# Starting the first products on the unnormed x, three-pass low-rank products, shorter token mixes and interleaved first FFN pairs in a one-layer hybrid encoder

## Chip, cores and metric

One core of a Trainium2 chip (trn2). The metric is the device time of one execution in microseconds (us). Three runs of the kernel before the change took 849.54 us in the median (849.13 to 849.97). A difference of under 0.2% (1.7 us) can't be told from no change here.

## The reference

One layer on x of 512 positions by 1024 channels, in float32: a norm, one input projection whose columns feed four mixers and their gates, an output projection, and a feed-forward network (FFN) with a width-3 convolution. Cut to what the change touches:

```python
def rms_norm(x, g):
    return x * rsqrt(mean(x * x, axis=-1) + 1e-6) * g

def rwkv7_mixer(z, mu, w0, w2, a0, a2, g2, ...):
    z = z + (token_shift(z) - z) * mu          # token_shift: the row of the position before
    r, k, v, xw, xa, xg = split(z)             # 256, 256, 256, 64, 64, 128 columns
    decay = exp(-c * sigmoid(w0 + tanh(xw) @ w2))
    a = sigmoid(a0 + xa @ a2)
    g = sigmoid(xg) @ g2
    ...
def layer(x):
    h = rms_norm(x, mix_norm_g)
    proj = h @ w_in                            # 1024 x 7424
    x = x + mixers_and_gates(proj) @ w_o
    h2 = rms_norm(x, ffn_norm_g)
    up = causal_dwconv(h2 @ w_up, conv_w)      # three taps over positions
    gate, val = split(up)
    return x + (silu(gate) * val) @ w_down
```

## The kernel before

Activations stand in SBUF transposed, channels on the partitions and the 512 positions on the free axis, in tiles of 128 positions. Every large product is float32 by three passes of fp32r: each operand is split into a rounded part and its rest (`split`: ScalarE casts the first, VectorE subtracts for the second), and `mm3` issues hi by hi, hi by rest, rest by hi into one PSUM bank. Weights come in pieces of 128 x 512 (raw, then `whi` and `wlo`) on SyncE's DMA queue, in rings of a few buffers. A unit is 1024 rows by 256 weight columns: four pieces, two banks, 48 products of 512 columns. TensorE's order is written by hand. Side work (norms, the RWKV part, attention) runs as generators that `tick()` advances, one step per some number of `mm3` calls; the constants YA, YN, Y0, WN, WO are these numbers.

The start: `load_x` brings x in tiles x0 to x3 of 128 positions. Twelve warm-up products (L232) run on TensorE. ScalarE sums the squares of a tile (L239), VectorE makes 1/rms and a diagonal matrix of it, and TensorE multiplies x by the diagonal (L300), which turns and norms at once; VectorE multiplies by the norm's gain (L248, `hf`), `split` makes hH and hL. Only then do the products of the first units begin, on positions 0 to 255 (256 columns): the unit of the low-rank inputs, that of k and r, that of v. Tiles 2 and 3 are normed on ScalarE, turned (L348) and split in between, and the units' products on positions 256 to 511 follow into the other half of the same banks (`first_units`). L366 and L367 turn the small vectors, L368 copies them out of PSUM.

The token mix (`mixed`) copies a bank out by ScalarE, and VectorE takes the difference of neighbouring positions and adds mu times it. The low-rank products (L464, L466, L468 in `rwkv_half`) are plain float32: two of 64 rows and one of 128, for each of two halves of the RWKV channels.

The FFN: of the four tiles normed by `norm_to_h`, the last goes through a diagonal product (L219) and the others through transposes (L221). `up_pair` computes a gate and a value column block, the first pair on positions 0 to 255 and then 256 to 511, the others at 512 columns. `conv` reads each bank three times: ScalarE (L1097), then VectorE (L1098 and L1099). Four banks of the kind `mm` serve these products in turn, so that pair n+2 needs the banks of pair n.

Of the kernel before, what the change touches and what calls it, by code (L numbers as in the profile page):

```python
# [9 lines left out]
F32 = mybir.dt.float32  # L10
# [5 lines left out]
P = 128  # L16
# [35 lines left out]
def hybrid_encoder_layer(  # L52
# [150 lines left out]
    def norm_to_h(np_, xs, gb, st, tt, early, wait=1, tag="mm"):  # L203

        ss, sq, xn = st
        rs = norm_factor(ss)
        if early:
            dg = np_.tile([P, P], F32, tag="diag", name="diag", bufs=2)
            vec.tensor_scalar(out=dg, in0=ident, scalar1=rs, scalar2=None, op0=ALU.mult)
        else:  # L210
            for hf in range(2):
                vec.scalar_tensor_tensor(out=xn[:, half_of(hf)], in0=xs[:, half_of(hf)], scalar=rs, in1=gb[hf], op0=ALU.mult, op1=ALU.mult)
        yield wait
        for half in range(2):
# [10 lines left out]
    def gain(xn, xs, gb, hf):  # L225
        vec.tensor_tensor(out=xn[:, half_of(hf)], in0=xs[:, half_of(hf)], in1=gb[hf], op=ALU.mult)
# [8 lines left out]
    mix_rs, mix_pt = {}, {}  # L235

    def mix_sums(tt):
        ss, sq, _ = norm_start(npool)
        act.activation(out=sq, in_=x0[tt], func=AF.Square, accum_out=ss[:, 0:1])  # L239
        return ss  # L240

    def mix_factor(tt, ss):
        mix_rs[tt] = norm_factor(ss, 1)

    def mix_gain(tt, half):

# [43 lines left out]
    sp.dma_start(out=stackB, in_=fcw[0:P])  # L290
    with tc.manual_schedule(engines={mybir.EngineType.PE, mybir.EngineType.Activation, mybir.EngineType.DVE}):
        for tt in range(2):
            mix_factor(tt, mix_sums(tt))
            dg = npool.tile([P, P], F32, tag="diag", name="diag", bufs=2)
            vec.tensor_scalar(out=dg, in0=ident, scalar1=mix_rs[tt], scalar2=None, op0=ALU.mult)
            for half in range(2):
                mix_pt[tt, half] = pt = bank()
# [893 lines left out]
```

## Time and profile before

| | before |
|---|---|
| median of 3 runs | 849.54 us |
| the profiled execution | 849.13 us |
| its span on the chip | 847.4 us |
| TensorE busy | 838.4 us, 99% of the span |
| VectorE busy | 516.4 us, 61% |
| ScalarE busy | 378.3 us, 45% |
| DMA | 82.19 MB, 97 GB/s |

The span leaves 1.73 us of the execution around it. Busy shares are averages over the whole span; the engine whose share is near 100% sets the time, and only the stretches in which it waits, and its own work, can change it.

### The profile page before, as it was taken

The page shows a single profiled execution, that of the slowest core. Times are in us where ns is not written, and L with a number is a line of the kernel's source. Part 1 is how long each engine was busy: PE and PEld are TensorE (multiplying, and loading weights), DVE is VectorE, ACT ScalarE, POOL GpSimd, SP SyncE. Part 2 cuts the span into 40 slices and gives each one's busy share as a digit, 9 for nine tenths or more (in the row PEclk, how much of TensorE's full clock was granted, in tenths as well). Part 3 has the DMA queues.
Part 4 walks back from the last instruction along what each step waited for, and adds up shares of the span by engine and source line. Part 5 has one row for each costly group of instructions (what it writes and reads, how often), then busy time and mean ns, then how long its engine had stood idle before and what let it go on. Part 6 is the DMA issues. An engine that isn't in the chain of part 4 may idle for free.

```text
span 847.4 us, 12633 instructions
## 1 busy us (share of the span) xinstructions
PE 838.4 (99%) x4759; PEld 697.2 (82%) x4759; DVE 516.4 (61%) x890; ACT 378.3 (45%) x646; POOL 11.7 (1%) x53
## 2 busy tenths in 40 slices
PE   8999999999999999999999999999999999999997
PEld 8988888788878888888888888888888888888886
DVE  5577974796466577754565866626665366634645
ACT  6474444752326554534344554405442244413434
POOL 2000100000000000000000000000000000000000
PEclk9999999999999999999999999999999999999999
DMA  8323331224213322263355333305332153302102
GB/s 252 114 63 100 106 101 51 63 79 114 65 54 98 100 62 75 87 211 100 97 169 182 113 112 99 100 1 187 99 100 63 61 165 99 100 26 66 46 1 99
DMA packets 102772, 82.19 MB, mean 97 GB/s; under 512 B 12716, under 2 KB 91640, under 8 KB 102712
## 3 DMA queue, kind: packets, MB, share of 16 engines
q1 hardware_dynamic: 101880, 79.56, 31.5%
q10 hardware_dynamic: 752, 1.58, 0.6%
q8 instruction: 37, 0.61, 0.3%
q0 software_dynamic: 80, 0.26, 0.1%
q14 instruction: 23, 0.19, 0.1%
HBM read 78.88 MB, written 2.49 MB: 96 GB/s over the span
## 4 chain that ended last, share of the span: by engine, by line
PE 95%; DVE 2%; ACT 1%; DMA 1%; issue 1%; ACTq 0%; DVEq 0%
PE mm L178 26%; PE mm L179 26%; PE mm L180 25%; PE wk L179 3%; PE wk L180 3%; PE wk L178 3%; PE wk L596 1%; PE wk L968 1%; PE wk L1000 1%; PE wk L990 1%; DMA x<-in_x_dram 0%; PE wk L540 0%; DMA raw<-in_w_down_dram 0%; PE wk L566 0%; PE wk L683 0%
## 5 line engine op out<-in xcount | busy, mean ns | idle before, releaser
L109 ACT CAST whi<-raw 128x512 fp32r<-128x512 f32 x272 | 166.7, 622 | 306.4 <-PE mm L179 178.8
L106 DVE TENSOR_TENSOR wlo<-raw,whi 128x512 fp32r<-128x512 f32 x276 | 187.1, 687 | 156.9 <-ACT whi L109 155.0
L178 PE MATMUL mm<-hH,whi 128*128 128x512 f32 (+1 forms) x432 | 166.4, 385 | 0.5 <-ACT hH L318 0.5
L179 PE MATMUL mm<-hL,whi 128*128 128x512 f32 (+1 forms) x432 | 161.6, 374 | 0.3 <-DVE hL L106 0.3
L180 PE MATMUL mm<-hH,wlo 128*128 128x512 f32 (+1 forms) x432 | 161.8, 374 | 0.0
L179 PE MATMUL mm<-h2L,whi 128*128 128x512 f32 (+1 forms) x368 | 139.9, 380 | 0.5 <-DVE h2L L106 0.5
L178 PE MATMUL mm<-h2H,whi 128*128 128x512 f32 (+1 forms) x368 | 140.0, 380 | 0.0
L180 PE MATMUL mm<-h2H,wlo 128*128 128x512 f32 (+1 forms) x368 | 139.8, 380 | 0.0
L178 PEld LDWEIGHTS mm<-hH,whi 128*128 128x128 f32 x432 | 81.3, 188 | 15.8 <-ACT hH L318 0.7
L180 PEld LDWEIGHTS mm<-hH,wlo 128*128 128x128 f32 x432 | 81.3, 188 | 14.9
L179 PEld LDWEIGHTS mm<-hL,whi 128*128 128x128 f32 x432 | 81.4, 188 | 14.3 <-DVE hL L106 0.5
L179 PEld LDWEIGHTS mm<-h2L,whi 128*128 128x128 f32 x368 | 69.2, 188 | 13.7 <-DVE h2L L106 0.7
L178 PEld LDWEIGHTS mm<-h2H,whi 128*128 128x128 f32 x368 | 69.2, 188 | 13.1
L180 PEld LDWEIGHTS mm<-h2H,wlo 128*128 128x128 f32 x368 | 69.2, 188 | 13.1
L180 PE MATMUL mm<-whi,aL 128*128 128x512 f32 (+1 forms) x92 | 35.5, 386 | 0.0
L178 PE MATMUL mm<-whi,aH 128*128 128x512 f32 (+1 forms) x92 | 35.5, 385 | 0.0
L179 PE MATMUL mm<-wlo,aH 128*128 128x512 f32 (+1 forms) x92 | 35.4, 385 | 0.0
L1098 DVE SCALAR_TENSOR_TENSOR ga<-mm,vecs,ga 128x511 f32<-128x511 f32 x22 | 16.5, 750 | 29.3 <-ACT ga L1097 29.3
L180 PE MATMUL wk<-whi,aL 128*128 128x512 f32 (+1 forms) x88 | 33.8, 385 | 0.0
L179 PE MATMUL wk<-wlo,aH 128*128 128x512 f32 (+1 forms) x88 | 33.8, 384 | 0.0
L178 PE MATMUL wk<-whi,aH 128*128 128x512 f32 (+1 forms) x88 | 33.8, 384 | 0.0
L1066 DVE TENSOR_TENSOR xt<-xt,mm 128x512 f32<-128x512 f32 x16 | 11.0, 688 | 31.9 <-PE mm L180 31.9
(336 smaller groups left out, 1169.3 us busy)
## 6 DMA issues: line engine op xcount, KB each, us to landing
raw<-in_w_in_dram SPq DMA_DIRECT2D x104, 256.0 KB
raw<-in_w_up_dram SPq DMA_DIRECT2D x176, 128.0 KB
raw<-in_w_down_dram SPq DMA_DIRECT2D x44, 256.0 KB
raw<-in_w_o_dram SPq DMA_DIRECT2D x16, 256.0 KB
x<-in_x_dram SPq DMA_DIRECT2D x4, 512.0 KB
raw<-in_w_in_dram SPq DMA_DIRECT2D x16, 128.0 KB
xt<-in_x_dram SPq DMA_DIRECT2D x4, 512.0 KB
out_dram<-xn SPq DMA_DIRECT2D x7, 256.0 KB
```

The costliest lines, as they stand in the source:

```text
L106: vec.tensor_tensor(out=lo, in0=src, in1=hi.bitcast(F32), op=ALU.subtract)
L109: act.copy(hi, src)
L178: pe.matmul(ps, lhsT=sh, rhs=mh, start=first, stop=False)
L179: pe.matmul(ps, lhsT=sh, rhs=ml, start=False, stop=False)
L180: pe.matmul(ps, lhsT=sl, rhs=mh, start=False, stop=last)
L596: pe.matmul(ps[us, i * 64:i * 64 + 64], lhsT=lt, rhs=rh, start=True, stop=True)
L968: pe.matmul(zb[b][:, o:o + QW[ti]], lhsT=qS[j][:, hp, ti * P:(ti + 1) * P], rhs=k_[j][:, hp, 0:QW[ti]], start=n == 0 and ti != 0, stop=n = ...
L990: pe.transpose(out=ab[b][:, o:o + P], in_=az[:, QOF[ti] + si * P:QOF[ti] + (si + 1) * P], identity=ident)
L1000: pe.matmul(po[:, si * P:T], lhsT=vS[j][:, hp, si, :], rhs=a_[:, cols], start=(si == 0 and n == 0), stop=(si == 3 and n == 1))
L1066: vec.tensor_tensor(out=xt[:, tt, half_of(hf)], in0=xt[:, tt, half_of(hf)], in1=bk, op=ALU.add)
L1098: vec.scalar_tensor_tensor(out=t0[:, 1:T], in0=ps[:, 0:T - 1], scalar=ffc(1, i), in1=t0[:, 1:T], op0=ALU.mult, op1=ALU.add)
```

## The change

- x comes in halves of 512 channels, the first weight pieces between them. TensorE turns the tiles x0 and x1 as they come (L254); ScalarE multiplies by the gain while it casts (`first_hi`), VectorE makes the rest (`first_lo`): fH and fL, without the norm. The first three units' products on positions 0 to 255 use these. The first two units go pass by pass (`one_pass`), the order of the units is low-rank, v, then k and r.
- The factors 1/rms of x0 and x1 come later: two products of ones by the diagonals (L406) lay them out as a row over 256 positions, L407 copies the row, and six VectorE multiplications (L410) scale the left halves of the six banks in place. x0 to x3 are normed in place, turned (L395) and split for all later units. There are seven warm-up products instead of twelve.
- The mix is one ScalarE instruction (scale 1 - mu, from PSUM) and one VectorE instruction (mu times the neighbour, from PSUM).
- The low-rank products become three passes of fp32r with split operands (L507, L509); those of the second half move into the first half's step that waits YA. Their weights are loaded by SyncE with the small vectors.
- The FFN's last tile is turned by transposes like the others, with a wait of its own (WO2), and the first two pairs run interleaved at 256 columns on all four banks (`first_pairs`).

```diff
-YN = 5
+YN = 7
 YV = 4
-Y0 = 8
-WN = 20
-WN2 = 10
+Y0 = 10
+WN = 17
+WN2 = 4
+WN3 = 12
+WN4 = 8
+WN5 = 4
 ND = 3
 FN = 4
-NWARM = 12
+NWARM = 7
 WO = 10
+WO2 = 20
...
+    for tt in range(2):
+        load_x(tt, half_of(0))
...
+    fH = npool.tile([P, KT, 256], F32R, name="fH")
+    fL = npool.tile([P, KT, 256], F32R, name="fL")
...
+    def mix_norm(tt):
+        ss = small.tile([P, 4], F32, tag="ss", name="ss")
+        sq = npool.tile([P, D], F32, tag="sq", name="sq", bufs=1)
         act.activation(out=sq, in_=x0[tt], func=AF.Square, accum_out=ss[:, 0:1])
-        return ss
-
-    def mix_factor(tt, ss):
-        mix_rs[tt] = norm_factor(ss, 1)
-
-    def mix_gain(tt, half):
-
-        hf_ = npool.tile([P, 4, P], F32, tag="hf", name="hf", bufs=4)
-        vec.tensor_tensor(out=hf_, in0=mix_pt[tt, half].rearrange("p (k t) -> p k t", k=4),
-                          in1=gT_mix[:, half * 4:half * 4 + 4, :].broadcast_to([P, 4, P]), op=ALU.mult)
...
+    def first_turn(q):
+        pt = bank("wk")
+        for k in range(2):
+            for tt in range(2):
+                kt = 2 * q + k
+                pe.transpose(out=pt[:, (2 * k + tt) * P:(2 * k + tt + 1) * P], in_=x0[tt][:, kt * P:(kt + 1) * P], identity=ident)
+        return pt
+
+    def first_hi(pt, q, k):
+        kt = 2 * q + k
+        act.activation(out=fH[:, kt, :], in_=pt[:, 256 * k:256 * k + 256], func=AF.Copy, scale=gT_mix[:, kt, :])
+
+    def first_lo(pt, q, k):
+        kt = 2 * q + k
+        vec.scalar_tensor_tensor(out=fL[:, kt, :], in0=pt[:, 256 * k:256 * k + 256], scalar=gT_mix[:, kt, :], in1=fH[:, kt, :].bitcast(F32), op0=ALU.mult, op1=ALU.subtract)
...
-    first = col_unit(w_in_v, RW0 + 768, get=load_piece)
+    first = col_unit(w_in_v[:, 0:KT // 2], RW0 + 768, get=load_piece)
+    for tt in range(2):
+        load_x(tt, half_of(1))
+    first += col_unit(w_in_v[:, KT // 2:KT], RW0 + 768, get=load_piece)
     wslots[:] = [(wA, NRA, NWA)]
-    second = col_unit(w_in_v[:, 0:KT // 2], RW0 + 256, RW0, get=load_piece)
+    second = col_unit(w_in_v, RW0 + 512, get=load_piece)
+    wslots[:] = [(npool, 8, 8)]
+    third = col_unit(w_in_v[:, 0:KT // 2], RW0 + 256, RW0, get=load_piece)
     load_x(2)
-    second += col_unit(w_in_v[:, KT // 2:KT], RW0 + 256, RW0, get=load_piece)
     load_x(3)
-    wslots[:] = [(npool, 8, 8)]
-    third = col_unit(w_in_v, RW0 + 512, get=load_piece)
+    third += col_unit(w_in_v[:, KT // 2:KT], RW0 + 256, RW0, get=load_piece)
...
+    def one_pass(n, u, ps, h):
+
+        wn, m = ((0, fH), (0, fL), (1, fH))[n]
+        for kt in range(2 * h, 2 * h + 2):
+            for ci in range(2):
+                pe.matmul(ps[ci][:, 0:256], lhsT=u[h][wn][:, kt % 2, ci * P:(ci + 1) * P], rhs=m[:, kt, :], start=n == 0 and kt == 0, stop=n == 2 and kt == KT - 1)
+                if n == 2:
+                    tick()
...
+        u, ps = unit_w[0], unit_ps[0]
+        pt = [first_turn(0), first_turn(1)]
+        first_hi(pt[0], 0, 0)
+        act.copy(w[0][1], w[0][0])
+        first_hi(pt[0], 0, 1)
+        vec.tensor_copy(w[1][1], w[1][0])
+        for k in range(2):
+            first_hi(pt[1], 1, k)
+        for h in range(2):
+            one_pass(0, u, ps, h)
+        for q in range(2):
+            for k in range(2):
+                first_lo(pt[q], q, k)
+        pt += [first_turn(2), first_turn(3)]
+        for h in range(2):
+            one_pass(1, u, ps, h)
+        for h in range(2):
+            lo_of(*w[h])
+        for h in range(2):
+            one_pass(2, u, ps, h)
...
+    def mix_rest():
+        for tt, wait in ((2, WN), (3, WN2), (0, WN3), (1, WN4)):
+            yield wait
...
+            turned.append(tt)
+            if tt == 3:
+                mix_norm(0)
+                mix_norm(1)
+        yield WN5
+        pr = bank("wk")
+        for tt in range(2):
+            pe.matmul(pr[:, tt * P:(tt + 1) * P], lhsT=ones_f, rhs=mix_dg[tt], start=True, stop=True)
+        vec.tensor_copy(rs_row, pr[:, 0:256])
+        for ps in unit_ps:
+            for bk in ps:
+                vec.tensor_tensor(out=bk[:, 0:256], in0=bk[:, 0:256], in1=rs_row, op=ALU.mult)
...
+        u, ps = unit_w, unit_ps
+        for h in range(0, 4, 2):
+            for n in range(3):
+                for i in range(2):
+                    one_pass(n, u[1], ps[1], h + i)
         ps.append([bank("wk"), bank("wk")])
-        gemm2_part(u[2], ps[2], 0)
+        gemm2_part(u[2], ps[2], 0, h=(fH, fL))
+        while len(turned) < 2:
+            finish("norm", 1)
...
-        zs = rp.tile([P, T + 1], F32, tag="zs", name="zs", bufs=2)
-        pool.memset(zs[:, 0:1], 0.0)
-        act.copy(zs[:, 1:T + 1], ps)
-        d = rp.tile([P, T], F32, tag="zd", name="zd")
-        vec.tensor_tensor(out=d, in0=zs[:, 0:T], in1=zs[:, 1:T + 1], op=ALU.subtract)
+
         zm = rp.tile([P, T], F32, tag=nm, name=nm, bufs=bufs)
-        vec.scalar_tensor_tensor(out=zm, in0=d, scalar=col("mu", mi), in1=zs[:, 1:T + 1], op0=ALU.mult, op1=ALU.add)
+        act.activation(out=zm, in_=ps, func=AF.Copy, scale=keep_mu[:, mi:mi + 1])
+        vec.scalar_tensor_tensor(out=zm[:, 1:T], in0=ps[:, 0:T - 1], scalar=col("mu", mi), in1=zm[:, 1:T], op0=ALU.mult, op1=ALU.add)
...
-        pw = bank("wk")
-        pe.matmul(pw, lhsT=w2a2[0:64, cj], rhs=lora[0:64, :], start=True, stop=True)
-        pa = bank("wk")
-        pe.matmul(pa, lhsT=w2a2[64:P, cj], rhs=lora[64:P, :], start=True, stop=True)
-        pg = bank("wk")
-        pe.matmul(pg, lhsT=g2[:, cj], rhs=xg, start=True, stop=True)
...
+            pw, pa, pg = bank("wk"), bank("wk"), bank("wk")
+            for n, (a, b) in enumerate(((0, 0), (0, 1), (1, 0))):
+                for ps, rows_ in ((pw, slice(0, 64)), (pa, slice(64, P))):
+                    pe.matmul(ps, lhsT=lw[rows_, a, cj], rhs=lx[rows_, b, :], start=n == 0, stop=n == 2)
+            for n, (a, b) in enumerate(((0, 0), (0, 1), (1, 0))):
+                pe.matmul(pg, lhsT=lw[:, 2 + a, cj], rhs=lx[:, 2 + b, :], start=n == 0, stop=n == 2)
...
+        if j == 0:
+            lora_products(1)
...
-            spawn("norm", norm_to_h(fpool, xt[:, tt, :], gb, sts[tt], tt, tt == NT - 1, WO))
+            spawn("norm", norm_to_h(fpool, xt[:, tt, :], gb, sts[tt], tt, WO2 if tt == NT - 1 else WO, "mm" if tt < 2 else "wk"))
...
+    def first_pairs():
+
+        wslots[:] = [inA] * 7 + [inB]
+        n_piece[0] = 0
+        u = [up_cols(i) for i in range(2)]
+        ps = [[bank(), bank()] for _ in range(2)]
+        for n in range(2):
+            gemm2_part(u[n], ps[n], 0)
+        finish("norm")
+        for hs in ((0, 1), (2, 3)):
+            for n in range(2):
+                gemm2_part(u[n], ps[n], 1, hs)
+        return ps
...
+        begun = first_pairs() if a == 0 else []
         for i in range(n):
             wslots[:] = [inA]
-            up_pair(a + i)
+            up_pair(a + i, begun[i] if i < len(begun) else gemm2(up_cols(a + i)))
```

**VectorE at the place where the small vectors are copied out.** Names: hf is a turned tile times the gain, hL its rest, wlo the rest of a weight piece. Before:

```order
L248 TENSOR_TENSOR hf_425<-wk_420,gT_mix_111 128x512 [waits PE_49]
L106 TENSOR_TENSOR wlo_726<-raw_724,whi_725 128x512 [waits DMAHW2_49,Activation_49]
L106 TENSOR_TENSOR hL_94<-hf_416,hH_93 128x4x128 [waits Activation_49]
L106 TENSOR_TENSOR hL_94<-hf_425,hH_93 128x4x128 [waits Activation_49]
L106 TENSOR_TENSOR wlo_732<-raw_730,whi_731 128x512 [waits DMAHW3_49]
L106 TENSOR_TENSOR wlo_738<-raw_736,whi_737 128x512 [waits DMAHW4_49]
L368 COPY vecs_288<-wk_485 128x256 [waits PE_49]
```

After, the same place:

```order
L397 TENSOR_TENSOR hf_532<-wk_527,gT_mix_106 128x512 [waits PE_49]
L397 TENSOR_TENSOR hf_541<-wk_536,gT_mix_106 128x512 [waits PE_49]
L110 TENSOR_TENSOR hL_94<-hf_532,hH_93 128x4x128 [waits Activation_49]
L110 TENSOR_TENSOR wlo_773<-raw_771,whi_772 128x512 [waits DMAHW2_49,PE_49,Activation_49]
L110 TENSOR_TENSOR hL_94<-hf_541,hH_93 128x4x128 [waits Activation_49]
L407 COPY rs_row_110<-wk_557 128x256 [waits PE_49]
L428 COPY vecs_320<-wk_567 128x256 [waits PE_49]
L410 TENSOR_TENSOR mm_189<-mm_189,rs_row_110 128x256 [waits DVE_49]
L410 TENSOR_TENSOR mm_190<-mm_190,rs_row_110 128x256
L410 TENSOR_TENSOR mm_191<-mm_191,rs_row_110 128x256
L410 TENSOR_TENSOR mm_192<-mm_192,rs_row_110 128x256
```

Here the split of tile x1 (the first five rows), the copies and the multiplications of the banks stand in one queue; two more multiplications, of wk_373 and wk_374, follow.

**TensorE at the same place**, in the second halves of the first units (mm_296 and mm_297 before; mm_191 and mm_192 after are the banks of v). Before:

```order
L180 MATMUL mm_296<-hH_93,wlo_114 128x256
L367 MATMUL wk_485<-ident_88,stackB_182 128x128 [waits DMAHW1_49]
L178 MATMUL mm_296<-hH_93,whi_113 128x256
L179 MATMUL mm_296<-hL_94,whi_113 128x256
L180 MATMUL mm_296<-hH_93,wlo_114 128x256
```

After:

```order
L395 MATMUL wk_536<-ident_88,x0_86 128x128 x3
L182 MATMUL mm_192<-hH_93,whi_130 128x256
...
L182 MATMUL mm_191<-hH_93,whi_134 128x256
...
L406 MATMUL wk_557<-diag_436,ones_f_77 128x128 [waits DVE_49]
L406 MATMUL wk_557<-diag_446,ones_f_77 128x128
...
L427 MATMUL wk_567<-ident_88,stackB_183 128x128 [waits DMAHW3_49]
L182 MATMUL mm_192<-hH_93,whi_134 128x256 [waits DVE_49]
```

Between the last transpose of tile x1 and the row that waits for VectorE stand 12 products of 256 columns (6 into mm_192, 6 into mm_191), the two factor products and the two vector transposes. What that last row waits for is the multiplication of mm_192.

**VectorE and TensorE at the first FFN pairs** (mm_4895, mm_4896 are pair 0's banks; mm_4897, mm_4898 pair 1's; mm_5207, mm_5208 pair 2's, the same memory as pair 0's; wlo_5285, 5292, 5299 belong to pair 3; before, mm_4836 and mm_4837 are pair 0's banks). VectorE before:

```order
L106 TENSOR_TENSOR wlo_5109<-raw_5107,whi_5108 128x512 [waits PE_49,Activation_49]
L1098 SCALAR_TENSOR_TENSOR ga_4970<-mm_4836,vecs_288,ga_4970 128x511 [waits Activation_49]
L106 TENSOR_TENSOR wlo_5116<-raw_5114,whi_5115 128x512 [waits DMAHW1_49,DMAHW2_49,PE_49,Activation_49]
L1099 SCALAR_TENSOR_TENSOR ga_4970<-mm_4836,vecs_288,ga_4970 128x510 [waits DVE_49]
L1098 SCALAR_TENSOR_TENSOR va_4975<-mm_4837,vecs_288,va_4975 128x511 [waits Activation_49]
L1099 SCALAR_TENSOR_TENSOR va_4975<-mm_4837,vecs_288,va_4975 128x510 [waits DVE_49]
```

VectorE after:

```order
L110 TENSOR_TENSOR wlo_5285<-raw_5283,whi_5284 128x512 [waits DMAHW0_49,DMAHW1_49,PE_49,Activation_49]
L1148 SCALAR_TENSOR_TENSOR ga_5127<-mm_4895,vecs_320,ga_5127 128x511 [waits Activation_49]
L110 TENSOR_TENSOR wlo_5292<-raw_5290,whi_5291 128x512 [waits DMAHW2_49,DMAHW3_49,PE_49,Activation_49]
L1149 SCALAR_TENSOR_TENSOR ga_5127<-mm_4895,vecs_320,ga_5127 128x510 [waits DVE_49]
L1148 SCALAR_TENSOR_TENSOR va_5132<-mm_4896,vecs_320,va_5132 128x511 [waits Activation_49]
L110 TENSOR_TENSOR wlo_5299<-raw_5297,whi_5298 128x512 [waits DMAHW4_49,DMAHW5_49,PE_49,Activation_49]
L1149 SCALAR_TENSOR_TENSOR va_5132<-mm_4896,vecs_320,va_5132 128x510 [waits DVE_49]
```

TensorE after:

```order
L184 MATMUL mm_4896<-h2H_4551,wlo_4862 128x256
L182 MATMUL mm_4897<-h2H_4551,whi_4882 128x256
...
L184 MATMUL mm_4898<-h2H_4551,wlo_4890 128x256
L182 MATMUL mm_5207<-h2H_4551,whi_5180 128x512 [waits DVE_49,Activation_49]
...
L182 MATMUL mm_5208<-h2H_4551,whi_5180 128x512 [waits DVE_49,Activation_49]
```

VectorE has one more split between pair 0's two last reads; between pair 0's last product and pair 2's first one TensorE has 24 products of 256 columns, where pair 1's whole unit (48 products of 512 columns) stood before between pair 0's and pair 2's.

## Rows read from the trace of the kernel before

**Rows 1.** The page: busy time of each engine, and TensorE's granted clock in 40 slices.

```profile
PE 838.4 (99%) x4759; PEld 697.2 (82%) x4759; DVE 516.4 (61%) x890; ACT 378.3 (45%) x646; POOL 11.7 (1%) x53
PEclk9999999999999999999999999999999999999999
```

**Rows 2.** TensorE's waits: line waited for, us in total, times, longest.

```profile
PE wk L232 <- DVE ones_f L86: 1.3, 1, 1.3
PE mm L178 <- ACT hH L318: 0.5, 1, 0.5
PE mm L179 <- DVE h2L L106: 0.5, 1, 0.5
PE mm L179 <- DVE hL L106: 0.3, 1, 0.3
```

**Rows 3.** Timeline of the start: start us, us, engine, line, out<-in, count, idle before.

```profile
1.25 5.44 PE L232 MATMUL wk<-ones_f 128*128 128x128 f32 x24 [1.25 <-DVE ones_f L86]
4.88 1.06 ACT L239 ACTIVATE sq<-x 128x1024 f32<-128x1024 f32 x1 [1.95 <-DMA x<-in_x_dram]
7.17 3.84 PE L300 MATMUL mm<-diag,x 128*128 128x128 f32 x32 [0.32 <-DVE diag L295]
11.54 0.38 PE L178 MATMUL mm<-hH,whi 128*128 128x256 f32 x1 [0.54 <-ACT hH L318]
12.27 0.39 PE L179 MATMUL mm<-hL,whi 128*128 128x256 f32 x1 [0.34 <-DVE hL L106]
```

**Rows 4.** Windows: stretch, us, busy of PE, PEld, DVE, ACT, POOL, granted clock.

```profile
12.27:48.37 36.10, 36.10 (x306) 36.10 (x307) 19.62 (x34) 17.94 (x32) 0.19 (x4) 1.00 0.43 129
```

**Rows 5.** Groups by form, 0 to 50 us: count, busy us, mean ns of one.

```profile
L106 DVE TENSOR_TENSOR wlo<-raw,whi 128x512 fp32r<-128x512 f32 x19 | 12.4, 686 | 14.4 <-ACT whi L109 14.4
L109 ACT CAST whi<-raw 128x512 fp32r<-128x512 f32 x15 | 8.5, 615 | 14.9 <-PE mm L179 14.9
L368 DVE COPY vecs<-wk 128x256 f32<-128x256 f32 x1 | 0.4, 425 | 0.7 <-PE wk L367 0.7
```

**Rows 6.** Groups by form, whole span: 256 columns out of PSUM.

```profile
L694 DVE TENSOR_TENSOR Yt<-wk,Yt 128x256 f32<-128x256 f32 x4 | 1.5, 418 | 1.4 <-PE wk L692 1.4
L109 ACT CAST aH<-wk 128x256 fp32r<-128x256 f32 x4 | 1.5, 373 | 5.8 <-PE wk L990 5.8
```

**Rows 7.** Timeline of the first half's low-rank products on TensorE.

```profile
53.90 0.39 PE L179 MATMUL mm<-hL,whi 128*128 128x512 f32 x1
54.13 0.39 PE L180 MATMUL mm<-hH,wlo 128*128 128x512 f32 x1
54.45 0.69 PE L464 MATMUL wk<-lora,w2a 64*128 64x512 f32 x1
54.45 0.69 PE L466 MATMUL wk<-lora,w2a 64*128 64x512 f32 x1
...
56.70 0.40 PE L179 MATMUL mm<-hL,whi 128*128 128x512 f32 x1
```

**Rows 8.** Timeline of the FFN's start on TensorE.

```profile
478.58 1.03 PE L221 MATMUL mm<-ident,xn 128*128 128x128 f32 x8
479.57 0.28 PE L179 MATMUL mm<-h2L,whi 128*128 128x256 f32 x1
483.06 2.02 PE L219 MATMUL mm<-diag,xn 128*128 128x128 f32 x16
485.04 0.28 PE L179 MATMUL mm<-h2L,whi 128*128 128x256 f32 x1
```

**Rows 9.** Timeline at the end of pair 0: TensorE's last product into the gate's bank, ScalarE, VectorE.

```profile
491.63 0.28 PE L180 MATMUL mm<-h2H,wlo 128*128 128x256 f32 x1
491.96 0.69 ACT L1097 ACTIVATE ga<-mm,vecs 128x512 f32<-128x512 f32 x1 [0.22 <-PE mm L180]
492.68 0.75 DVE L1098 SCALAR_TENSOR_TENSOR ga<-mm,vecs,ga 128x511 f32<-128x511 f32 x1 [0.22 <-ACT ga L1097]
495.38 0.75 DVE L1099 SCALAR_TENSOR_TENSOR va<-mm,vecs,va 128x510 f32<-128x510 f32 x1
```

More of the change, by code (lines that the diff above doesn't have):

```diff
@@ L290, in hybrid_encoder_layer @@
     sp.dma_start(out=stackB, in_=fcw[0:P])
-    with tc.manual_schedule(engines={mybir.EngineType.PE, mybir.EngineType.Activation, mybir.EngineType.DVE}):
[L292 to L295, printed above, removed]
+    lw_f = const.tile([P, 2, 256], F32, name="lw_f")
+    sp.dma_start(out=lw_f[0:64, 0, :], in_=rw_w2[0])
@@ new lines, in one_pass @@
+    def one_pass(n, u, ps, h):
[5 more added lines that the diff above has]
+                    tick()
+    unit_w = [[hl for _, hl in w] for w in (first, second, third)]
+    unit_ps = [[bank(), bank()], [bank(), bank()]]
+    with tc.manual_schedule(engines={mybir.EngineType.PE, mybir.EngineType.Activation, mybir.EngineType.DVE}):
+        w = [raw_hi_lo for raw_hi_lo, _ in first]
+        u, ps = unit_w[0], unit_ps[0]
[18 more added lines that the diff above has]
+            one_pass(2, u, ps, h)
+        for q in (2, 3):
+            for k in range(2):
+                first_hi(pt[q], q, k)
+            act.copy(w[q][1], w[q][0])
+        for h in (2, 3):
+            one_pass(0, u, ps, h)
+        for q in (2, 3):
+            for k in range(2):
+                first_lo(pt[q], q, k)
+        for h in (2, 3):
+            one_pass(1, u, ps, h)
+        for h in (2, 3):
+            lo_of(*w[h])
+        for h in (2, 3):
+            one_pass(2, u, ps, h)
+        for raw_hi_lo, _ in second:
+            split(*raw_hi_lo)
+        for raw_hi_lo, _ in third[0:2]:
+            split(*raw_hi_lo)
+        mix_norm(2)
+        mix_norm(3)
+        for raw_hi_lo, _ in third[2:4]:
+            split(*raw_hi_lo)
@@ L296, in hybrid_encoder_layer @@
+    turned = []
+    def mix_rest():
+        for tt, wait in ((2, WN), (3, WN2), (0, WN3), (1, WN4)):
+            yield wait
             for half in range(2):
[L297 removed]
+                pt = bank("wk")
                 for k in range(4):
                     ks = slice((half * 4 + k) * P, (half * 4 + k + 1) * P)
[L300 to L301 removed]
@@ L302, in hybrid_encoder_layer @@
-        mix_xn = {}
-        def mix_norm(tt, ss):
-            mix_factor(tt, ss)
-            mix_xn[tt] = npool.tile([P, D], F32, tag="xn", name="xn", bufs=2)
-            act.mul(mix_xn[tt], x0[tt], mix_rs[tt])
-        w = [raw_hi_lo for raw_hi_lo, _ in (first[0], first[1], second[0], second[1], first[2], first[3], second[2], second[3])]
-        for n in range(2):
-            act.copy(w[n][1], w[n][0])
-        s0 = mix_gain(0, 0)
-        act.copy(s0[1], s0[0])
-        lo_of(*w[0])
-        s1 = mix_gain(1, 0)
@@ L335, in hybrid_encoder_layer @@
[L335 to L350 removed]
+                    pe.transpose(out=pt[:, k * P:(k + 1) * P], in_=x0[tt][:, ks], identity=ident)
@@ L444, in rwkv_half @@
             yield 1
-        cj = slice(j * P, (j + 1) * P)
         def t2(tag, nm=None, bufs=1):
```

172 lines of the change are left out of this document (67 added, 105 removed).

## The prediction

> **What bounds the kernel now.** I read the page first. TensorE is busy for 838.4 us of a span of 847.4 and its granted clock is at full speed in every slice [rows 1], so the time is TensorE's own work plus its waits. Then the list of its waits: after the start's 1.3 us they are one of 0.5 and one of 0.3 before the first products, and one of 0.5 in the FFN [rows 2]. So only three things can move the time: when the first product starts, how much work TensorE has, and waits that the change makes. VectorE at 61% and ScalarE at 45% [rows 1] matter where TensorE waits for their order, not for their sum.
>
> The timeline of the start shows what the first product waits for: x lands (the sum of squares starts at 4.88), then norm, diagonal product, split; the first product is at 11.54, the second at 12.27 [rows 3]. From there to the first 512-column product at 48.37 TensorE is busy without a gap: 306 instructions in 36.10 us, 0.118 us each [rows 4]. Those are 288 products of 256 columns, 16 transposes and 2 vector transposes.
>
> **The start.** The first half-megabyte is now the two left halves of x, in place of one whole tile, so they should land at about 4.88 as that tile did [rows 3]. Eight transposes follow. At the slow clock of the warm-ups (5.44 us for 24, 0.23 each) they take 1.8 us, at the later pace (3.84 for 32, 0.12) 1.0 [rows 3]. ScalarE's first gain (0.37 from PSUM [rows 6]) and first weight cast (0.62 [rows 5]) run beside them, so the first product starts at about 6.9 (6.2 to 7.5). Work from there: 288 x 0.118 = 34.0; 40 transposes (8 of x's right halves, 32 for the later tiles) at 0.111, 4.4; factor products (4 passes of 0.11) 0.45; vector transposes 0.22. Sum 39.1. In the first unit ScalarE has eight gains and three casts (4.8 us), VectorE eight rests at 0.42 [rows 6], four at 0.69 and one cast of some 0.5 (6.6 us), against TensorE's 6.7, each half in strict passes behind them: I charge 0.9 for the gaps (0 to 2). The end of the stage would be 6.9 + 39.1 + 0.9 = 46.9, against 48.37: **-1.5**.
>
> **A new wait at the banks.** The six multiplications by the factors write the left halves of banks whose right halves are then filled. The order shows that TensorE's second group into mm_192 waits until VectorE has multiplied mm_192. Count from the start of tile x1's second-last set of turns. TensorE's cover is 8 transposes (0.9), 12 products (1.4), factors 0.45, vectors 0.22: it is at the waiting product after 3.0 us. VectorE's queue cannot be there by then: the first four transposes end after 0.5; two gains of 0.6 each run to 1.8; ScalarE casts one half, a weight piece, then the other half (3 x 0.62, to 3.2); the second rest, 0.65, ends at 3.85; row copy, vector copy and four multiplications, 6 x 0.36 (0.42 of each [rows 5, 6] less the overlap), end at about 6.1. So **TensorE stops for 3.1 us**. It is at least 2.1 (the copies and four multiplications alone begin after the factor products, 2.9, and take 2.2), at most 3.6. Behind the wait come mm_192's, then k's and r's banks, whose multiplications are by then one step ahead, so it is paid once. In the trace of before no instruction of VectorE writes a bank that is still to be filled; there the copy L368 held nobody. The Trainium skill ("PSUM — Partial Sum Buffer", section on bank collisions) says that two engines must not touch one bank's partitions at a time, even in other columns, so this wait cannot be taken as mere caution; by that rule too the sum is +3.1, and without it, if the halves could overlap, 0.
>
> **Clock.** Seven warm-ups end near 4.2 where twelve ended near 6.7 [rows 3]. I charge 0.3 for transposes and products that still run at the slow pace.
>
> **Low-rank products.** Before: from the product at 54.13, whose successor would be at 54.36, to the one at 56.70, which would have started at 56.47 without a break, 2.1 us; the two of 64 rows start at the same time, 54.45 [rows 7]. After: three passes of such pairs and three of the full one, 6 x 0.23 (a 512-column product's pace, 53.90 to 54.13 [rows 7]) = 1.4, and 0.1 of change-over: -0.65, and twice, since the second half's are the same: **-1.3**. Bounds: 0 (the pairs don't overlap: nine products, 2.1) and -1.5. Moving the second half's products earlier changes only their place; the splits of operands (8 instructions on ScalarE and VectorE) lie beside 512-column units.
>
> **The mixes** leave 8 VectorE instructions of 0.69 and 8 on GpSimd out, and read PSUM by ScalarE and VectorE. No wait of TensorE comes from them now [rows 2], so I cost them at nothing; what hides them is the SC unit's 11 us. If the banks of the first mix were late, SC's second bank would wait, 0.1 to 0.7.
>
> **FFN.** The wait of 0.5 [rows 2] goes, because the last tile is turned after two more half units. Its diagonal product took 483.06 to 485.04 less one product, 1.86; turns take 478.58 to 479.57 less one product, 0.87 [rows 8]: -1.0. Pair 1 runs as 96 products of 0.12 instead of 48 of 0.23: +0.5. Then pair 2's first product needs pair 0's banks with a cover of only 24 x 0.12 = 2.9 us where 11 stood. Before, ScalarE began 0.33 after TensorE's last start in the gate's bank and VectorE's last read of the value's bank ended at 496.13, 4.2 us after ScalarE began [rows 9]. With that chain, and one more split of 0.6 in it, the gate's bank is free 2.3 us after pair 0's last product, inside the cover, and the value's bank at 4.3, where TensorE arrives at 2.9 + 1.4: **0.15** of waiting (0 to 1.75, if the weight pieces of pair 3, which stand ahead in both queues, land late). Sum -0.85.
>
> **Total:** -1.5 + 3.1 + 0.3 - 1.3 - 0.85 = -0.25 us. Against the profiled execution's 849.13 that is 848.9; the median lies 0.4 above it, which gives 849.3. I forecast 849.1, no change that can be told.
>
> **Rivals.**
>
> 1. *Slower, by the clock.* The first unit runs in short passes between waits. If TensorE's clock, which before is at full speed for the products of the diagonals at 7.17 (0.12 each against 0.23) [rows 3], rises only when the first unit is nearly through, the 48 products and 8 turns of that unit take 0.23 each instead of 0.12, up to +6 of work, of which 3 to 4 hide in gaps that I charged or in waits for the two other engines: +2.5, 851.6. It decides from a rise after about 12 us. Against it: the warm-ups still run. The Trainium skill ("TensorE: Matmul & The Clock Gate", part 4) holds that transposes do not count as busy work for the clock as products do, which speaks against a start on transposes; by that page alone the time would be this 851.6. In the trace of before the turns at 478.58 come between products at full clock [rows 8], which does not test it.
> 2. *Faster, because the start is tight and the wait short.* If VectorE gets to the copies as soon as the factor products are done (2.1 instead of 3.1), and the first unit has no gaps and no slow clock (-0.9, -0.3), the sum is -2.45: 846.7. For it: VectorE is busy for only 19.62 of the 36.10 us of that stage [rows 4]. Against: the chain through ScalarE. It decides from a bank wait under 2.3.
> 3. *The FFN banks.* The wait there at its upper bound, +1.6: 850.7.
> 4. *The low-rank products do not get shorter*, since pairs of fp32r passes do not overlap: +1.3, 850.4.
>
> **How the numbers follow.** Forecast 0.43 (own range 847.9 to 850.9), rival 1 0.19, rival 2 0.25, rival 3 0.08 (half of it beyond 851.2, with other small losses), rival 4 0.05. A fifth on either side is left out by 846.3 to 852.0. Faster than 847.84: rival 2 and the lower edge of the forecast, 0.27. Slower than 851.24: rival 1 and half of rival 3, 0.23. The rest, 0.50, is no change. The 0.2% is 1.7 us.
>
> **What would show it.** First product at 6.2 to 7.5. A TensorE wait for VectorE's L410 of about 3.1 us near 35 to 38. The first 512-column product at 50.3. Low-rank products of about 1.4 us each time, the 64-row ones starting in pairs. No wait for h2L in the FFN, and at most a few tenths at pair 2. I am wrong if the bank wait is under 2 us or absent, if the first unit ends after 15 us, or if a wait stands elsewhere.

## The result and the profile after

The changed kernel takes 855.61 us in the median of 6 runs (854.87 to 857.11), against 849.55 for six runs of the kernel before beside them: a ratio of 1.0076 (1.0066 to 1.0087). It is slower by some 6 us, and above the forecast range. The profiled execution took 855.34 us with a span of 853.6, 6.2 more than the span before, 847.4.

The page of the kernel after, busy times by engine and the granted clock in 40 slices:

```profile
PE 840.0 (98%) x4799; PEld 699.9 (82%) x4799; DVE 519.5 (61%) x904; ACT 382.6 (45%) x657; POOL 11.0 (1%) x45
PEclk9999999999999999999999999999999999999999
```

TensorE is busy for 1.6 us more than in [rows 1] and waits for the rest. The clock's line shows nothing: a slice is 21 us long, and a digit of 9 still covers a few microseconds at half clock. The list of TensorE's waits (line waited for, us in total, times, longest) against [rows 2]:

```profile
PE mm L182 <- DVE mm L410: 2.8, 1, 2.8
PE mm L182 <- DVE scx L845: 2.0, 1, 2.0
PE wk L225 <- DVE ones_f L90: 1.3, 1, 1.3
PE mm L334 <- DVE whi L347: 0.5, 1, 0.5
PE mm L183 <- DVE hL L110: 0.4, 1, 0.4
```

The first row is the bank wait that was forecast. The second was not forecast at all. To see how much each stretch lost I compared the start of three products in both traces:

| stretch | before | after | difference |
|---|---|---|---|
| to the first 512-column product | 48.21 | 53.44 | +5.23 |
| from there to the FFN's first product | 429.30 | 431.08 | +1.78 |
| from there to the FFN's last product | 363.62 | 362.60 | -1.02 |
| the rest of the span | | | +0.24 |

**The start.** Timeline of the kernel after (start us, us, engine, line, out<-in, count, idle before):

```profile
4.75 1.97 PE L254 MATMUL wk<-ident,x 128*128 128x128 f32 x8
6.27 0.61 ACT L345 CAST whi<-raw 128x512 fp32r<-128x512 f32 x1
6.93 0.88 PE L334 MATMUL mm<-fH,whi 128*128 128x256 f32 x4 [0.22 <-ACT whi L345]
7.71 0.43 DVE L347 CAST whi<-raw 128x512 fp32r<-128x512 f32 x1 [2.69 <-DMA raw<-in_w_in_dram]
8.28 0.59 PE L334 MATMUL mm<-fH,whi 128*128 128x256 f32 x3 [0.47 <-DVE whi L347]
```

The turns begin when x lands, and the first product starts at 6.93 where before it started at 11.54 [rows 3]. The second weight piece is late: VectorE waits 2.69 for it, and TensorE then 0.47 for VectorE.

**The bank.** The same view around 38 us:

```profile
36.98 0.68 DVE L110 TENSOR_TENSOR hL<-hf,hH 128x512 fp32r<-128x512 f32 x1
37.59 0.42 DVE L407 COPY rs_row<-wk 128x256 f32<-128x256 f32 x1
37.92 0.41 DVE L428 COPY vecs<-wk 128x256 f32<-128x256 f32 x1
38.25 1.42 DVE L410 TENSOR_TENSOR mm<-mm,rs_row 128x256 f32<-128x256 f32 x4
39.72 0.39 PE L182 MATMUL mm<-hH,whi 128*128 128x256 f32 x1 [2.84 <-DVE mm L410]
```

VectorE is without a gap from the split to the fourth multiplication, and TensorE's first product into that bank starts when the fourth ends. Windows of this stretch (start:end, us, busy and count of PE, PEld, DVE, ACT, POOL, granted clock, DMA share, GB/s):

```profile
36.70:39.70 3.00, 0.18 (x2) 0.00 (x0) 3.00 (x9) 0.08 (x1) 0.00 (x0) 1.00 0.31 87
39.70:44.20 4.50, 4.48 (x25) 4.48 (x26) 1.39 (x4) 0.62 (x1) 0.00 (x0) 0.63 0.17 52
44.20:48.00 3.80, 3.80 (x34) 3.80 (x34) 0.00 (x0) 0.00 (x0) 0.16 (x3) 0.99 0.02 7
```

The wait itself is about 3.0 us. Then, a microsecond after TensorE has begun again, the granted clock falls to half (1.2 of 2.4 GHz): the list of its products shows a pace of 0.12 us up to 40.78, of 0.214 from 40.93 to 44.14 (15 steps in 3.21), and of 0.12 again. That costs another 1.5 us in which TensorE counts as busy, so no list of waits shows it.

**The short-convolution (SC) unit.** Timeline around the second wait:

```profile
94.44 0.40 PE L184 MATMUL mm<-whi,hL 128*128 128x512 f32 x1
94.57 0.67 DVE L606 TENSOR_TENSOR AoT<-MT,omask 64x512 f32<-64x512 f32 x1
95.17 0.99 DVE L601 TENSOR_REDUCE dc<-dg 128x128 f32<-128x512 f32 x1
96.09 1.27 DVE L845 TENSOR_TENSOR scx<-mm,scc 128x512 f32<-128x512 f32 x2
96.82 0.50 PE L182 MATMUL mm<-whi,hH 128*128 128x512 f32 x1 [1.98 <-DVE scx L845]
```

A unit begins to fill a bank that L845 has yet to read, and L845 stands on VectorE behind a chain of the RWKV part (L589, L598, L606, L601) from 89.88 on. The step from 94.44 to 96.82 is 2.38 us where a product's pace is 0.23: 2.15 lost. In the order the RWKV step that issues L587, the products ahead of this chain, comes after 141 product triples and before after 137; the SC unit ends at 144 in both. Its chain now lies over the unit's end.

**Low-rank products**, to be read against [rows 7]:

```profile
60.70 0.39 PE L184 MATMUL mm<-hH,wlo 128*128 128x512 f32 x1
61.02 0.98 PE L507 MATMUL wk<-lx,lw 64*128 64x512 f32 x6
61.93 0.97 PE L509 MATMUL wk<-lx,lw 128*128 128x512 f32 x3
62.73 0.39 PE L182 MATMUL mm<-hH,whi 128*128 128x512 f32 x1
```

From 60.70 to 62.73, less one product of 0.23, they take 1.80, against 2.11 before. The six of 64 rows do overlap in pairs: 0.91 for three pairs.

**The FFN**, where pair 1 ends and pair 2 begins:

```profile
509.12 0.28 PE L184 MATMUL mm<-h2H,wlo 128*128 128x256 f32 x1
509.25 0.40 PE L182 MATMUL mm<-h2H,whi 128*128 128x512 f32 x1
509.48 0.39 PE L183 MATMUL mm<-h2L,whi 128*128 128x512 f32 x1
```

Pair 2 starts without a wait, and the wait for h2L of [rows 2] is gone from the list.

### The profile page after: what moved, and what is told of

Its sections match the earlier page's. It is cut to its first block, busy times and chain, and to the rows that moved or that the text cites. A ratio compares the mean times of both kernels' runs of the same rounds, so it can differ in the third digit from the quotient of the medians.

```text
span 853.6 us, 12713 instructions
## 1 busy us (share of the span) xinstructions
PE 840.0 (98%) x4799; PEld 699.9 (82%) x4799; DVE 519.5 (61%) x904; ACT 382.6 (45%) x657; POOL 11.0 (1%) x45
## 4 chain that ended last, share of the span: by engine, by line
PE 94%; DVE 1%; ACT 0%; issue 0%
PE mm L182 26%; PE mm L184 25%; PE mm L183 25%; PE wk L184 3%; PE wk L182 3%; PE wk L183 3%; PE wk L643 1%; PE wk L1020 1%; PE wk L1052 1%; PE wk L1042 1%; PE wk L730 0%; PE wk L587 0%; PE wk L613 0%; DVE MT L589 0%; PE wk L703 0%; PE wk L711 0%
## 5 line engine op out<-in xcount | busy, mean ns | idle before, releaser
L182 PE MATMUL mm<-hH,whi 128*128 128x512 f32 (+1 forms) x400 | 156.6, 392 | 2.8 <-DVE mm L410 2.8
L183 PE MATMUL mm<-hL,whi 128*128 128x512 f32 (+1 forms) x400 | 152.7, 382 | 0.4 <-DVE hL L110 0.4
L184 PE MATMUL mm<-hH,wlo 128*128 128x512 f32 (+1 forms) x400 | 152.6, 382 | 0.0
L182 PE MATMUL mm<-h2H,whi 128*128 128x512 f32 (+1 forms) x384 | 142.8, 372 | 0.0
L182 PEld LDWEIGHTS mm<-hH,whi 128*128 128x128 f32 x400 | 75.1, 188 | 18.0 <-DVE mm L410 3.1
L184 PEld LDWEIGHTS mm<-hH,wlo 128*128 128x128 f32 x400 | 75.1, 188 | 14.9
L183 PEld LDWEIGHTS mm<-hL,whi 128*128 128x128 f32 x400 | 75.2, 188 | 13.9 <-DVE hL L110 0.6
L182 PEld LDWEIGHTS mm<-h2H,whi 128*128 128x128 f32 x384 | 72.3, 188 | 12.8 <-ACT ga L1171 0.3
L183 PEld LDWEIGHTS mm<-h2L,whi 128*128 128x128 f32 x384 | 72.3, 188 | 12.5
L184 PEld LDWEIGHTS mm<-h2H,wlo 128*128 128x128 f32 x384 | 72.3, 188 | 12.4
```

The source lines that it names most:

```text
L182: pe.matmul(ps, lhsT=sh, rhs=mh, start=first, stop=False)
L183: pe.matmul(ps, lhsT=sh, rhs=ml, start=False, stop=False)
L184: pe.matmul(ps, lhsT=sl, rhs=mh, start=False, stop=last)
```

## The experiments

My theory after this reading: the loss is made by two waits with a cause each, the multiplications L410 in VectorE's order (3.0, and 1.5 of clock that follows from the idle time) and the RWKV step's new place (2.15). The rivals: that the slow stretch belongs to the products or transfers there and not to the idle time; that the wait at L845 is late because everything ahead of it is late, not because of the step's place; and that the start loses by itself. Times beside each run are medians, with the ratio to the kernel before on the same chip (849.2 in the first four, 849.3 to 849.4 in the others).

**1. Without the multiplications.**

```diff
-        for ps in unit_ps:
-            for bk in ps:
-                vec.tensor_tensor(out=bk[:, 0:256], in0=bk[:, 0:256], in1=rs_row, op=ALU.mult)
```

> The changed kernel without the six multiplications of the banks by the factors (the first 256 positions of six banks stay unnormed). Theory A, the multiplications hold TensorE and the idle time lets its clock fall: the wait of 2.8 us and the slow products behind it both go, the first 512-column product starts at 48.8 instead of 53.4, the time falls by 4.6 us to about 851.0, and the wait for L845 near 94 stays. Rival, the slow products come from something else in that stage (the transposes, the short products): only the wait goes, 3.0 us, to about 852.6, with products at 0.21 us still there.

Measured: 850.41 us (849.73 to 852.35), ratio 1.0018 (1.0009 to 1.0027). The first 512-column product starts at 48.12. Its waits:

```profile
PE mm L182 <- DVE scx L842: 2.0, 1, 2.0
PE wk L225 <- DVE ones_f L90: 1.3, 1, 1.3
PE mm L334 <- ACT whi L345: 1.0, 1, 1.0
PE mm L334 <- DVE whi L347: 0.6, 1, 0.6
PE mm L183 <- DVE hL L110: 0.5, 1, 0.5
```

The bank wait is gone, and with it the slow stretch, in a window of the same time:

```profile
39.70:44.20 4.50, 4.50 (x40) 4.50 (x39) 0.00 (x0) 0.27 (x1) 0.27 (x3) 1.00 0.14 46
```

The SC wait (now L842) stays as it was although everything ahead of it is 5.3 us earlier, so lateness from the start is not its cause. And the start, freed of its wait, is at 48.12 only level with before (48.21): it gains nothing to speak of, with 2.1 us of waits for weights and hL.

**2. The idle time filled.** 26 products into a part of a bank that nobody reads, ahead of the vector transposes:

```diff
         pv = bank("wk")
+        for n in range(26):
+            pe.matmul(pv[:, 256:512], lhsT=unit_w[0][0][0][:, 0, 0:P], rhs=fH[:, n % 4, :], start=True, stop=True)
```

> The changed kernel with 26 useless products of 256 columns put in front of the vector transposes, into unused columns of their bank, so that TensorE works through the wait. Theory A: 26 x 0.12 = 3.1 us of work take the place of the wait, the clock does not fall, the products behind run at 0.12 us; the time falls by about 1.6 us to 854.0. Rival, the clock falls for another reason than the idle time: the slow stretch stays, time unchanged at 855.6.

Measured: 854.84 us (853.53 to 855.07), ratio 1.0063 (1.0048 to 1.0078); the first 512-column product at 51.60, 1.84 earlier than in the changed kernel. Windows over the filled wait and what follows:

```profile
36.80:40.00 3.20, 3.20 (x30) 3.20 (x29) 3.17 (x9) 0.00 (x0) 0.00 (x0) 1.00 0.33 82
40.00:44.00 4.00, 4.00 (x37) 4.00 (x35) 0.99 (x3) 0.62 (x1) 0.00 (x0) 1.00 0.21 65
```

The clock stays at 1.00 behind the filled gap. From the product that waited (here at 39.42, in the changed kernel at 39.72) to the first 512-column product it is 12.18 us in place of 13.72. In this pair of traces the slow stretch costs 1.54; the other 0.3 is that this run came to the bank earlier. That the idle time is its cause is likely from here and from experiment 1, where neither idle time nor slow stretch is left, but it is not shown: in experiment 9 below the wait stands unfilled and the clock stays up too. The medians don't show it either. The profiled run is the fastest of the four here; the others are 1.3 to 1.5 longer, at a mean granted clock of 0.996 against its 0.997, so their clock may have fallen somewhere, and no trace tells where.

**3. The RWKV step back to its place.**

```diff
-YN = 7
+YN = 5
-Y0 = 10
+Y0 = 8
```

> The changed kernel with YN 5 and Y0 8 as before. Theory S, the wait for L845 comes from the RWKV part's steps standing 4 product triples later against the third short-convolution unit, so that VectorE reaches L845 behind four masks and a reduction while TensorE has only 9 products left: the wait goes, minus 2.1 us, about 853.5. Rival, it comes from the second half's low-rank products that now stand in the first half's step: the wait stays, 855.6.

Measured: 854.05 us (852.83 to 854.65), ratio 1.0052 (1.0035 to 1.0069). Waits:

```profile
PE mm L182 <- DVE mm L410: 2.8, 1, 2.8
PE mm L334 <- ACT whi L345: 2.0, 1, 2.0
PE wk L225 <- DVE ones_f L90: 1.3, 1, 1.3
```

The SC wait is gone, and from the first 512-column product to the FFN it is 428.75, 2.33 less than in the changed kernel. So the place of the step, set by YN and Y0, is its cause; the rival is dead, because the second half's low-rank products still stand in the first half's step here. The median falls by only 1.6, and this run's trace shows why its own time is high: the first weight piece landed a microsecond later (2.0 of waiting), and the clock then fell twice, for 3.4 us after that wait and for 6.0 after the bank wait, this time from the first product on:

```profile
39.90:45.90 6.00, 6.00 (x28) 6.00 (x29) 1.34 (x4) 0.62 (x1) 0.00 (x0) 0.50 0.15 44
8.30:11.70 3.40, 3.40 (x17) 3.40 (x17) 2.86 (x8) 1.53 (x5) 0.00 (x0) 0.50 1.09 357
```

Up to the product at 7.91 this program is the same as the changed kernel; when the piece lands, and how long the clock stays down, differs from run to run. The four runs of this kernel spread over 1.8 us.

**4. The FFN part alone** (the kernel before with the last tile turned by transposes, WO2, and `first_pairs`):

```diff
-            spawn("norm", norm_to_h(fpool, xt[:, tt, :], gb, sts[tt], tt, tt == NT - 1, WO))
+            spawn("norm", norm_to_h(fpool, xt[:, tt, :], gb, sts[tt], tt, False, WO2 if tt == NT - 1 else WO, "mm" if tt < 2 else "wk"))
...
-            up_pair(a + i)
+            up_pair(a + i, begun[i] if i < len(begun) else gemm2(up_cols(a + i)))
```

> The kernel before with the FFN's part of the change alone (last tile by transposes, first two pairs interleaved). If the FFN's gain stands by itself: minus 1.0 us, 848.5 (the stage from the first FFN product to the last product 362.6 instead of 363.6). Rival, the gain in the changed kernel came from weight pieces that landed earlier through the delays before: 849.5, with a wait at pair 2's banks.

Measured: 848.17 us (847.77 to 848.22), ratio 0.9988 (0.9978 to 0.9997); FFN stage 362.62, as in the changed kernel (362.60). The FFN part is a gain of 1.0 and owes nothing to the rest of the change. It is under the 1.7 us of the metric; its interval just excludes no change, and the stage in the trace shows where it comes from.

**5. Multiplications later, step back.** Each bank is multiplied when its right half is done, so that nobody waits for it there; YN and Y0 as in 3:

```diff
                 gemm2_part(u[n], ps[n], 1, hs)
+                if hs == (2, 3):
+                    for bk in ps[n]:
+                        vec.tensor_tensor(out=bk[:, 0:256], in0=bk[:, 0:256], in1=rs_row, op=ALU.mult)
```

> The changed kernel with the six multiplications moved behind the right halves of their banks (each pair of banks when its unit is through), and YN 5, Y0 8 as before; it computes the same. If the two waits and the fall of the clock were the whole loss against before, the time falls by 5.0 + 2.1 us from the changed kernel's and stands about 1 us under the kernel before (low-rank products -0.6, FFN -1.0, the start +0.3 to +0.6): 0.999. Rival, a new wait at the mixes, which now stand behind the multiplications: up to +2, 1.001.

Measured: 849.87 us (849.24 to 850.74), ratio 1.0006 (0.9997 to 1.0016). Both waits are gone, but a new one has come, and the first 512-column product is at 49.88:

```profile
47.95 0.43 DVE L445 TENSOR_TENSOR wk<-wk,rs_row 128x256 f32<-128x256 f32 x1 [0.90 <-PE wk L184]
48.65 0.43 DVE L445 TENSOR_TENSOR wk<-wk,rs_row 128x256 f32<-128x256 f32 x1 [0.27 <-PE wk L184]
48.99 0.74 DVE L462 SCALAR_TENSOR_TENSOR KBx<-mm,vecs,KBx 128x511 f32<-128x511 f32 x1
49.88 0.47 PE L182 MATMUL mm<-hH,whi 128*128 128x512 f32 x1 [1.26 <-DVE KBx L462]
```

The last two multiplications wait for TensorE's last products, and the mixes, which free the bank for the SC unit, stand behind them in VectorE's order. This start, too, had a wait of 1.6 for the first weight piece and half clock until 11.2. That a start of this kind could gain without these is left open; I did not find an order that has neither wait.

**6. The start of before, with all the rest** (and YN 5, Y0 8, as before: the hunks of the FFN, the mixes and the low-rank products on the kernel before).

> The kernel before with all of the change but its start: three-pass low-rank products, shorter mixes, the FFN's part, YN 5 and Y0 8. By the stages read from the changed kernel's trace: -0.6 for the low-rank products, -1.0 for the FFN, no wait for the third short-convolution unit: 1.6 us under before, 0.998. By the prediction's term for the low-rank products (-1.3): 2.3 us under. Rival, the splits of the low-rank operands make a wait of their own there: 1 us under or less.

Measured: 848.28 us (847.91 to 848.42), ratio 0.9987 (0.9978 to 0.9996). First 512-column product 48.04, from there to the FFN 428.76, FFN 362.63; waits:

```profile
PE wk L233 <- DVE ones_f L87: 1.3, 1, 1.3
PE mm L179 <- ACT hH L323: 0.5, 1, 0.5
PE mm L180 <- DVE hL L107: 0.3, 1, 0.3
```

The median is 1.1 under the kernel before, where 1.6 were expected. With the start of before and the step in its place nothing of the loss remains. With experiment 4 it is the fastest version here. Its middle stage is 0.56 shorter than experiment 4's 429.32, which is what the low-rank products are worth in the trace; the two medians don't show it.

**7. The shorter mixes without the three-pass products** (experiment 4 and the new `mixed`):

```diff
-        zs = rp.tile([P, T + 1], F32, tag="zs", name="zs", bufs=2)
...
-        act.copy(zs[:, 1:T + 1], ps)
...
+        act.activation(out=zm, in_=ps, func=AF.Copy, scale=keep_mu[:, mi:mi + 1])
+        vec.scalar_tensor_tensor(out=zm[:, 1:T], in0=ps[:, 0:T - 1], scalar=col("mu", mi), in1=zm[:, 1:T], op0=ALU.mult, op1=ALU.add)
```

> The kernel before with the FFN's part and the shorter mixes, low-rank products as before. If the mixes are hidden as predicted: the FFN's -1.0 us alone, 0.9988. What the kernel with the low-rank products gains over this one is their price: -0.6 by the trace of the changed kernel, -1.3 by the prediction.

Measured: 849.56 us (849.46 to 849.69), ratio 1.0003 (0.9995 to 1.0012): 1.4 slower than experiment 4. The first 512-column product is at 49.25, against 48.22 there, and the middle stage is 429.31, as there. Timeline ahead of it (ACTq is the DMA issue on ScalarE):

```profile
46.98 0.61 ACTq L766 DMA_DIRECT2D g<-in_rw_g_dram  x1
47.64 0.69 ACT L419 ACTIVATE lora<-mm,keep_mu 128x512 f32<-128x512 f32 x1 [1.25 <-DVE wlo L107]
48.36 0.75 DVE L420 SCALAR_TENSOR_TENSOR lora<-mm,vecs,lora 128x511 f32<-128x511 f32 x1 [1.25 <-ACT lora L419]
49.25 0.47 PE L179 MATMUL mm<-hH,whi 128*128 128x512 f32 x1 [0.58 <-DVE lora L420]
```

Before, ScalarE's copy alone freed the bank; now VectorE reads it as well. ScalarE issues three low-rank weight loads (0.53 and 0.61 twice) just ahead of the first mix, and 0.6 of waiting comes out. In the changed kernel and in experiment 6 these loads are on SyncE's queue, and the wait is not there. The order of the first two mixes differs there too, so that the loads make the wait is read from the timelines and not tested alone. The rest of the 1.4 is not explained: about 0.4 of it comes ahead of this wait, the rest behind the last product.

**8 and 9. Small loads ahead of x's right halves.** Does the second weight piece land late because the transfers issued behind it share the DMA engines with it? Four (and eight) loads of 4 KB between the second piece and x's right halves push those back:

```diff
+    for n in range(4):
+        gap = npool.tile([8, P], F32, name="gap%d" % n)
+        sp.dma_start(out=gap, in_=w_in_v[0:8, 0, n * P:n * P + P])
     for tt in range(2):
         load_x(tt, half_of(1))
```

> The changed kernel with four tiny useless loads (4 KB each) issued between the second weight piece and x's right halves, so that those are issued some 1.5 us later. Theory L, the first two weight pieces share the DMA engines with what is issued right behind them: they land earlier than in the five runs with this start (casts of the second piece at 6.8 to 8.0 us), the second piece by about 6.5. Rival, the pieces take this long by themselves: its cast stays at 6.8 to 8.0.

> The same with eight tiny loads, x's right halves some 3 us later. Theory L: the second piece's cast at or below 6.5 again; the first unit then waits for x's right halves instead. Rival: its cast stays at 6.8 to 8.0.

Measured, one run each: 857.3 and 857.03 us. Timeline of VectorE's cast of the second piece, with four loads:

```profile
6.38 0.43 DVE L350 CAST whi<-raw 128x512 fp32r<-128x512 f32 x1 [1.35 <-DMA raw<-in_w_in_dram]
```

It comes at 6.38, and with eight at 6.62, against 6.76 to 7.96 in the five kernels without them (7.71 in the changed one). The piece landed earlier in both, but with one run each, and so close to the edge of what varies anyway (6.76), theory L is not shown. Nothing is won: with eight loads TensorE waits 1.8 for the halves of x, with four 1.7 for the copy of a later tile (`hf`). With eight, the bank wait was 3.2, and yet the clock stayed at full speed:

```profile
36.00:45.00 9.00, 5.79 (x49) 5.55 (x48) 6.50 (x16) 2.29 (x4) 0.15 (x1) 1.00 0.34 95
```

With four, the clock also fell behind the SC wait of 2.0:

```profile
98.40:101.80 3.40, 3.40 (x10) 2.66 (x9) 3.40 (x6) 1.34 (x3) 0.00 (x0) 0.50 0.28 82
```

## Why the prediction was wrong

By its own steps, in us of the span:

| step | forecast | measured |
|---|---|---|
| the start | -1.5 | +0.7 |
| the bank wait | +3.1 | +3.0 |
| clock | +0.3, at the start | +1.5, behind the bank wait |
| low-rank products | -1.3 | -0.6 |
| the move of the low-rank products, the mixes | 0 | 0 |
| the RWKV step counts YN and Y0 | no term | +2.15 |
| FFN | -0.85 | -1.0 |
| not traced further | | +0.5 |
| sum | -0.25 | +6.2 |

**The bank wait was right**, in its place, its chain and its size. The Trainium skill ("PSUM — Partial Sum Buffer", section on bank collisions) was cited for it. The trace shows that the program holds the product into the other half of the bank (39.72) until the fourth multiplication ends (39.67); whether the two could have overlapped, no run here shows.

**"So it is paid once" failed.** It holds for the wait and not for what follows it. I had looked for the clock at the start, after the shortened warm-ups, and never asked what three idle microseconds do in the middle of the stage. The runs showed 1.5 us at half clock behind it. In the trace of experiment 2, with the gap filled, the slow stretch is gone, which prices it at 1.54. The Trainium skill ("TensorE: Matmul & The Clock Gate", section "HAM oscillation — how this bites in real kernels") tells of a kernel whose TensorE waits for a DMA after each burst, is throttled again, and begins the next burst cold. The row of 39.70 to 44.20 agrees in part, with 0.63 granted: nine products still went at 0.12 before the clock fell, while in experiment 3 the first one was slow already, and in experiment 9 a longer wait cost no clock. It was this sentence of the Trainium skill that spoke to the change, and I weighed another one.

**Rival 1 is dead as it was put.** The clock rose between 6.7 and 8.3, on transposes and first products, in the changed kernel. But in experiments 3 and 5, where the first weight piece came later, it fell again until 11.7 and 11.2: its mechanism is real where a wait of 1.6 to 2.0 comes first. What the Trainium skill says of transposes ("TensorE: Matmul & The Clock Gate", part 4) is not tested by this start: seven warm-up products stand right ahead of the eight transposes, and in experiments 1, 2 and 5 the clock was up while the transposes ran (0.109 each; in the changed kernel 0.213).

**The step counts had no term**, and are the largest unpriced loss: 2.15. The change takes YN from 5 to 7 and Y0 from 8 to 10, in the first lines of its diff, and the sum puts that at nothing without a reason. I read the order for the instructions that the change moves, and not for the other steps of the same generator. Those came four triples later (141 in place of 137), and one of them puts a chain of 6 us on VectorE in front of the read that frees a bank. Experiments 3 and 6 show it: with the two counts back the wait is gone, in both. "Moving the second half's products earlier changes only their place" held: both experiments keep that move, and no wait comes of it.

**The start was mis-sized by 2.2.** Its first product at 6.9 was right. The stage end was not: the first 512-column product of before starts at 48.21, not 48.37 (0.16); products go at 0.120 each, not at the 0.118 of a mean with transposes in it (0.6 over 288); the waits behind the first product are 1.05 (0.47, 0.42 and 0.16), not 0.9. Of the other 1.3 I can say only that it lies in many short losses, steps of 0.14 to 0.28 where the pace is 0.12: in the first pass, behind waits, and where TensorE changes between turns and products. Experiment 1 shows the start without the bank wait: 48.12, no gain, where I had 46.9.

**The low-rank products were mis-sized**: 1.80 a half, not 1.45. Three pairs take 0.91 and three full passes 0.80, where 0.69 was charged for either: the steps at a change of form (0.32 to 0.34) and not the products make the difference. Rival 4 is dead, since the pairs do overlap.

**The FFN was right**, and so was its mechanism: transposes for the diagonal product, no wait at pair 2; rival 3 is dead. The 0.15 charged for the banks did not come; its own figures, free at 4.3 and needed at 2.9 + 1.4, gave none. Rival 2 fell with the bank wait, which was not under 2.3.

**The mixes cost nothing in the changed kernel, but not by the cover that I named.** I had 0.1 to 0.7 if the banks were late. Experiment 7 gives 0.6 where ScalarE still issues the low-rank loads, so what hides them is most likely that the change takes those loads off ScalarE.

**What stays open:** whether the new start can gain at all with both waits gone; the 0.5 of the last line but one, of which 0.2 goes with the step counts (2.33 in experiment 3, against the 2.15 of the wait); and why a wait of the same length costs the clock in one run and not in another. The changed kernel's six runs spread over 2.2 us. The two longest (856.59 and 857.11) have a mean granted clock of 0.994, the other four 0.996, which one more fall would explain; the one profile can't show where it lies.

## What to carry to other kernels

Price a wait of TensorE with its idle time and with the clock that may fall behind it, read from the rows of the stretch that follows, and where several microseconds of idle can't be avoided, try filling them. Where a step count of a generator is changed, look at every step that comes after it on the same counter, and at whose bank it then stands in front of. A change of several parts is worth cutting: here the parts that gained 1 us were hidden under a start that lost 5 and a step out of place that lost 2.

## What the hardware showed that I had not expected

The clock fell around waits of 1.6 to 3 us, at the start and in the midst of full work, and mostly stayed at half for 3.4 us, once for 6.8 (experiment 3, the first 0.8 of it inside the bank wait). It did not always fall: behind the bank wait it fell in the changed kernel, experiment 3 and experiment 8, but not in experiment 9, where the wait was 3.2; behind the SC wait of 2.0 it fell in experiments 8 and 9 and not in the changed kernel and experiments 1 and 2.

A piece of weights may land later when more is issued behind it, though it was issued first: its cast came at 6.38 and 6.62 with small loads in between, in one run each, and at 6.76 to 7.96 in the five profiles without.
